# Two fused model blocks: every SBUF tile moved to a whole line of 64 bytes, with shared buffers for queries and values

## The chip, the cores and the metric

The kernel runs on one core of a Trainium2 chip. The metric is the device time of one execution in microseconds (us). The time before is the median of three runs: 1470.78 us (1470.22 to 1472.76).

## The reference

Two blocks follow each other, in float32, on 256 tokens of width 1024, with 16 meta tokens ahead of them.

```python
# first block
proj = rms_norm(h, g) @ w_in                      # 1024 -> 5 * 512
y_sc = bg * conv3(cg * xv)
y_cf = silu(layer_norm(conv31(ga * sigmoid(gg)) + b))
h = h + concat(rms_norm(y_sc), rms_norm(y_cf)) @ w_out
q = rms_norm(h) @ w_q                             # 8 heads, two halves of 128
...                                               # top 16 of 128 x 128 experts by head, softmax gates
act = gelu(u_sel . x);  h = h + (act * gates) @ v_sel
# second block
sb_q, sb_k, sb_v, df_q, df_k, df_v = split(rmsnorm(h) @ w_in2)
...                                               # stick-breaking and differential attention, 8 heads each
h = h + (gates0 * (o_sb @ w_br_sb) + gates1 * (o_df @ w_br_df)) @ w_out2
h = h + (silu(hn @ w_fg) * (hn @ w_fu)) @ w_fd    # 22 slices of 128
```

The kernel computes all 16384 experts densely (`u` and `v` have 128 chunks of 128 rows each) and multiplies the activations by a gate matrix that is zero outside of the chosen ones.

## The kernel before, in words

**Weights and units.** All weights come in units of 128 x 1024 float32 (512 KB). SyncE loads a unit into one of five `raw` buffers (line 128), ScalarE rounds it to float32r as `hi` (line 150), VectorE computes the rest `lo = raw - hi` (line 152); `hi` and `lo` have three buffers each. A product is then three float32r matmuls: hi by hi, hi by lo, lo by hi.

**Two forms of product.** `mm_w` (lines 164 to 171) takes the unit as the stationary operand and the activations as the moving one: 8 chunks x 3 = 24 matmuls, each of 128 x 128 weights, with 256 moving columns (272 where the meta tokens count too). `mm_a` (lines 173 to 184) takes the activations as stationary and half a unit as moving: 12 matmuls of 512 columns. Counted from the loops:

- 512 columns: units of `v` (128), `w_fd` (22), `w_out` (8), `w_out2` (8), 12 matmuls each: 1536 + 456 = 1992.
- 256 columns with `hThi`/`hTlo` as moving operand: `u` (128), `w_q` (16), `w_fg` and `w_fu` (44): 188 units x 24 = 4512.
- 256 columns with other moving operands: gates (16), queries (16), the two branches (16, moving operands `osb` and `odf`), `bg` (4): 52 x 24 = 1248.
- 272 columns: `gg`, `ga`, `cg`, `xv` (16), keys and values (32): 48 x 24 = 1152.

Together 8904 of the 10096 matmul instructions. The others are plain float32: transposes, the convolution (`conv`, line 373), the gate matrix (`gp`, line 675), attention scores and sums (`z`, `S`, `po`). A plain float32 matmul is two instructions in the trace.

**Order.** TensorE and SyncE run in the order in which the program is written; a scheduler orders the other engines. While the expert units of `u` run, VectorE routes the tokens and later builds the gate matrix (about 390 to 590 us). `v` follows (600 to 945 us), then the second block.

**SBUF.** Tiles come from pools. `const` (line 55) lives to the end; each phase opens a pool of its own with `phase` (line 63), in whose space the next phase puts its tiles. A tile has the same address in all 128 partitions. In the program before, each tile is given the bytes that it needs in a partition, rounded up to 32, and the tiles lie one behind the other. `const` begins at a multiple of 64 with `vec`, `ones` and `eps`; `eps` is one float32, so that it takes 32 bytes, and what lies behind it begins 32 bytes past a multiple of 64. Of the 207 different places of tiles in this program 184 lie so and 23 at a multiple of 64. All moving operands of the 8904 float32r matmuls are among the 184, and all their stationary operands but those of 48 (the second half of `w_out`).

**Attention.** `feat` (line 882) makes queries, keys and transposed values, `value` (line 894) transposes a head's values back. Queries have the tags `sq` and `dq` with two buffers each, values `sv` and `dv` with two each, for the two kinds of attention, which run one after the other (lines 1008 and 1032).

Of the kernel before, what the change touches and what calls it, by code (L numbers as in the profile page):

```python
# [8 lines left out]
F32 = mybir.dt.float32  # L9
# [9 lines left out]
P = 128  # L19
# [27 lines left out]
NV = _n  # L47


@with_exitstack  # L50
def two_blocks(ctx, tc, x, feats, vecs, w_in, w_out, w_q, keys, u, v, final_g, meta2, w_in2, lams, w_gate,
               w_br_sb, w_br_df, w_out2, w_fg, w_fu, w_fd, final_g2, gains, out):
    nc = tc.nc

    const = ctx.enter_context(tc.tile_pool(name="const", bufs=1))
    wraw = ctx.enter_context(tc.tile_pool(name="wraw", bufs=5))
    whi = ctx.enter_context(tc.tile_pool(name="whi", bufs=3))
    wlo = ctx.enter_context(tc.tile_pool(name="wlo", bufs=3))
# [3 lines left out]

    def phase(name):
        st = ExitStack()
        pool = st.enter_context(tc.tile_pool(name=name, bufs=1, reuse_waits="tile"))
        return st, pool

    def mm_tile(name):
        return pmm.tile([P, 512], F32, tag="mm", name=name)
# [3 lines left out]
    def at_tile(name):  # L73
        turn[0] += 1
        return pacc.tile([P, 512], F32, tag=f"a{turn[0] % 4}", name=name)
# [88 lines left out]
    def mm_w(ps, a, cols):  # L164
        hi, lo = unit()
        ahi, alo = a
        for k in range(KC):
            ks = slice(k * P, (k + 1) * P)
            nc.tensor.matmul(ps, hi[:, ks], ahi[:, k, cols], start=(k == 0), stop=False)  # L169
            nc.tensor.matmul(ps, hi[:, ks], alo[:, k, cols], start=False, stop=False)  # L170
            nc.tensor.matmul(ps, lo[:, ks], ahi[:, k, cols], start=False, stop=(k == KC - 1))  # L171
# [125 lines left out]
    sq = pc.tile([P, KC, L], F32, tag="sq", name="sq")  # L297
# [423 lines left out]
    for hd in range(NH):  # L721
# [3 lines left out]
        for half in range(2):  # L725
            ps = mm_tile(f"q{hd}{half}")
            mm_w(ps[:, :T], hT, slice(0, T))
            q = pr.tile([P, T], F32, tag="qT", name=f"qT{hd}{half}", bufs=4)
# [115 lines left out]
    QS = slice(NM, L)  # L844
# [37 lines left out]
    def feat(name, hd, tag, cols, scale=1.0):  # L882
        width = cols.stop - cols.start
        ps = mm_tile(f"ps_{name}")
        mm_w(ps[:, :width], xT2, cols)

        def scaled():
            o = padded[tag][hd % len(padded[tag])] if tag in padded else psb.tile([P, width], F32, tag=tag, name=name, bufs=2)
            nc.vector.scalar_tensor_tensor(o[:, :width], ps[:, :width], scale, rsb[:, cols], op0=ALU.mult, op1=ALU.mult)
            return o  # L890

        return scaled

    def value(name, tag, vt):
        ps = at_tile(f"pv_{name}")
        o = psb.tile([P, 3, P], F32, tag=tag, name=name, bufs=2)
        for kt in range(3):
            nc.tensor.transpose(ps[:, kt * P:(kt + 1) * P], vt[:, kt * P:(kt + 1) * P], ident)
        nc.scalar.activation(o, ps[:, :KP].rearrange("p (a b) -> p a b", a=3), AF.Copy)
        return o  # L900

    def qcols(kt, j=None):
        j = kt if j is None else j
        return slice(QO[kt] + Q0[j] - Q0[kt], QO[kt] + QN[kt])

    def stick(hd, q, k, vT):
        pz = at_tile(f"z{hd}")
        for kt in range(3):
            nc.tensor.matmul(pz[:, qcols(kt)], k[:, kt * P:(kt + 1) * P], q[:, Q0[kt]:], start=True, stop=True)
        z = psb.tile([P, NQ], F32, tag="z", name=f"zs{hd}", bufs=2)  # L910
        nc.vector.tensor_tensor(z, pz[:, :NQ], mneg, op=ALU.add)
        e = psb.tile([P, NQ], F32, tag="e", name=f"e{hd}", bufs=2)
        nc.scalar.activation(e, z, AF.Abs)
        nc.scalar.activation(e, e, AF.Exp, scale=-1.0)
        nc.scalar.activation(e, e, AF.Ln, bias=1.0)
        nc.vector.scalar_tensor_tensor(e, z, 0.0, e, op0=ALU.max, op1=ALU.add)
        yield
        vt = value(f"sv{hd}", "sv", vT)
        yield
        yield  # L920
        ps = at_tile(f"S{hd}")
        for kt in range(3):
            for j in range(kt, 3):
                nc.tensor.matmul(ps[:, qcols(kt, j)], tri if j == kt else ones, e[:, qcols(j)],
                                 start=(j == kt), stop=(j == 2))
        nc.vector.tensor_tensor(z, z, ps[:, :NQ], op=ALU.subtract)
        nc.scalar.activation(z, z, AF.Exp)
        yield
        yield
        po = at_tile(f"po{hd}")  # L930
        for kt in range(3):
            nc.tensor.matmul(po[:, Q0[kt]:T], vt[:, kt, :], z[:, qcols(kt)], start=(kt == 0), stop=(kt == 2))
        nc.scalar.activation(osb[0][:, hd, :], po[:, :T], AF.Copy)
        nc.vector.tensor_tensor(osb[1][:, hd, :], po[:, :T], osb[0][:, hd, :].bitcast(F32), op=ALU.subtract)
# [3 lines left out]
    def diff(hd, q, k, vT):  # L938
        slope = 2.0 ** (-(hd + 1))
        ws = []  # L940
        for t in range(2):
            kn = KN[t]
            nm = psb.tile([P, 2], F32, tag="nm", name=f"nm{hd}{t}", bufs=2)
            sm = psb.tile([P, 2], F32, tag="dsm", name=f"dsm{hd}{t}", bufs=2)
            pe = []
            for c in range(2):
                cs = slice(64 * c, 64 * c + 64)
                ps = at_tile(f"ds{hd}{t}{c}")
                nc.tensor.matmul(ps[:, :kn], q[cs, t * P:(t + 1) * P], k[cs, :kn], start=True, stop=True)
                s = psb.tile([P, kn], F32, tag=f"ds{t}{c}", name=f"dss{hd}{t}{c}", bufs=2)  # L950
                nc.vector.scalar_tensor_tensor(s, dist[t], -slope, ps[:, :kn], op0=ALU.mult, op1=ALU.add)
                nc.vector.tensor_reduce(nm[:, c:c + 1], s, axis=AX.X, op=ALU.max, negate=True)
                nc.scalar.activation(s, s, AF.Exp, bias=nm[:, c:c + 1], accum_out=sm[:, c:c + 1])
                pe.append(s)
            nc.vector.reciprocal(sm, sm)
            nc.vector.tensor_scalar(pe[1], pe[1], sm[:, 1:2], lam, op0=ALU.mult, op1=ALU.mult)
            w = padded[f"w{t}"][0]
            nc.vector.scalar_tensor_tensor(w[:, :kn], pe[0], sm[:, 0:1], pe[1], op0=ALU.mult, op1=ALU.subtract)
            ws.append(w)
            if t == 0:  # L960
                yield
        vt = value(f"dv{hd}", "dv", vT)
        yield
        yield
        outs = []
        for t in range(2):
            nk = KW[t] // P
            pw = at_tile(f"pw{hd}{t}")
            wT = psb.tile([P, 3, P], F32, tag="wT", name=f"wT{hd}{t}", bufs=2)
            for i in range(nk):  # L970
                nc.tensor.transpose(pw[:, i * P:(i + 1) * P], ws[t][:, i * P:(i + 1) * P], ident)
            nc.scalar.activation(wT[:, :nk, :], pw[:, :KW[t]].rearrange("p (a b) -> p a b", a=nk), AF.Copy)
            outs.append(wT)
        yield
        for t, wT in enumerate(outs):
            nk = KW[t] // P
            po = at_tile(f"dpo{hd}{t}")
            for i in range(nk):
                nc.tensor.matmul(po[:, :P], wT[:, i, :], vt[:, i, :], start=(i == 0), stop=(i == nk - 1))
            nc.scalar.activation(od[t][:, hd, :], po[:, :P], AF.Copy)  # L980
# [22 lines left out]
    def advance():  # L1003
        for g in list(running):
            if next(g, running) is running:
                running.remove(g)

    for hd in range(NH):
        q = feat(f"sq{hd}", hd, "sq", QS, float(P) ** -0.5)
        if hd > 0:  # L1010
            q = q()
            advance()
        k = feat(f"sk{hd}", hd, "k", FULL)
        if hd > 0:
            k = k()
            advance()
        else:
            with tc.high_priority(offset=20):
                cols = x2_norm()
        vT = feat(f"svT{hd}", hd, "vT", FULL)  # L1020
        if hd == 0:
            with first():
                across(pb, cols, rsb[:, QS], "rsb")
            tc.keep_in_program_order(nc.scalar.preload_act_table_set("natural_log_exp_and_others"))
            q, k = q(), k()
        running.append(stick(hd, q, k, vT()))
        if hd > 0:
            advance()
        if hd == 0:
            with queued([latest["hi"], latest["lo"]]):  # L1030
                small_parts()
    for hd in range(NH):
        q = feat(f"dq{hd}", hd, "dq", QS, 0.125)()
        advance()
        k = feat(f"dk{hd}", hd, "k", FULL)()
        advance()
        vT = feat(f"dvT{hd}", hd, "vT", FULL)()
        running.append(diff(hd, q, k, vT))
        advance()
# [160 lines left out]
```

## Time and profile before

| | |
|---|---|
| median of the runs | 1470.78 us |
| the profiled execution | 1472.7 us |
| its span, first to last instruction | 1470.5 us |
| mean granted TensorE clock | 0.993 |
| busy: TensorE, its weight loads | 1440.7, 1341.6 us |
| busy: VectorE, ScalarE, GpSimd | 1052.5, 737.6, 14.7 us |
| DMA | 248.95 MB, mean 169 GB/s |

A matmul's duration in the trace includes its way through the array, and the next one starts before it ends. What a matmul costs in a row of matmuls is therefore the distance from its start to the next start, called its pace below: the starts of two rows, divided by the number of matmuls from the one to the other. The timeline gives starts to 0.01 us, so that a pace over 10 to 30 matmuls is good to about 1 ns. Two levels of the TensorE clock occur, 2.4 GHz (granted 1.00) and 1.2 GHz (0.50).

### The profile page before, as it was taken

What the parts mean: (1) busy time and instruction counts of PE and PEld (TensorE: products, weight loads), DVE (VectorE), ACT (ScalarE), POOL (GpSimd) and SP (SyncE); (2) the same over time, 40 slices, a digit from 0 to 9 for tenths busy, and PEclk for the clock granted to TensorE, in tenths of its full rate; (3) what the DMA queues carried; (4) which work ended last, traced back from release to release, by engine and by line L of the source; (5) the groups of instructions that cost most, each with busy time, mean ns of one, the idle gap of its engine ahead of it and who ended that gap; (6) DMA issues with size and microseconds to landing.
All of it is one profiled execution on the core that took longest, in us unless ns stands there. A gap on an engine that the chain in (4) does not pass through costs nothing.

```text
span 1470.5 us, 25555 instructions
## 1 busy us (share of the span) xinstructions
PE 1440.7 (98%) x10096; PEld 1341.6 (91%) x10096; DVE 1052.5 (72%) x1888; ACT 737.6 (50%) x1216; POOL 14.7 (1%) x35
## 2 busy tenths in 40 slices
PE   8999999999999999899999999999999999999998
PEld 7988999999999999688888888799999999899997
DVE  8987669679788999655555555665577776766665
ACT  7555444445444444244444444554455674544444
POOL 0010000000000000000000000100000000000000
PEclk9999999999999999999999999999999999999999
DMA  7525665665544444366666676553444455566562
GB/s 235 201 73 186 194 190 175 204 189 169 176 144 144 143 138 138 106 194 198 191 193 193 198 245 192 180 160 127 129 129 130 129 172 187 167 190 189 186 188 99
DMA packets 69815, 248.95 MB, mean 169 GB/s; under 512 B 7744, under 2 KB 9152, under 8 KB 69696
## 3 DMA queue, kind: packets, MB, share of 16 engines
q1 hardware_dynamic: 68544, 243.13, 52.6%
q0 software_dynamic: 1152, 4.19, 0.8%
q8 instruction: 79, 1.29, 0.4%
q14 instruction: 40, 0.33, 0.1%
HBM read 245.20 MB, written 2.10 MB: 168 GB/s over the span
## 4 chain that ended last, share of the span: by engine, by line
PE 94%; DVE 3%; DMA 1%; issue 1%; ACT 0%; SPq 0%; POOL 0%; DVEq 0%; ACTq 0%
PE u L171 8%; PE u L169 8%; PE u L170 8%; PE v L184 8%; PE v L183 8%; PE v L182 8%; PE gp L675 4%; PE fg L170 1%; PE fu L171 1%; PE fg L171 1%; PE fd L184 1%; PE fu L170 1%; PE fu L169 1%; PE fg L169 1%; PE fd L183 1%; PE fd L182 1%
## 5 line engine op out<-in xcount | busy, mean ns | idle before, releaser
L152 DVE TENSOR_TENSOR lo<-raw,hi 128x1024 fp32r<-128x1024 f32 x453 | 553.6, 1224 | 243.6 <-ACT hi L150 241.9
L150 ACT ACTIVATE hi<-raw 128x1024 fp32r<-128x1024 f32 x453 | 479.0, 1059 | 467.6 <-PE u L170 123.7
L169 PE MATMUL u<-hThi,hi 128*128 128x256 f32 x1024 | 290.5, 284 | 0.0
L171 PE MATMUL u<-hThi,lo 128*128 128x256 f32 x1024 | 285.7, 279 | 0.1
L170 PE MATMUL u<-hTlo,hi 128*128 128x256 f32 x1024 | 285.5, 279 | 0.0
L182 PE MATMUL v<-hi,w_hi 128*128 128x512 f32 x512 | 200.5, 392 | 1.3 <-ACT w_hi L764 1.3
L184 PE MATMUL v<-hi,w_lo 128*128 128x512 f32 x512 | 200.6, 392 | 0.5 <-DVE w_lo L766 0.5
L183 PE MATMUL v<-lo,w_hi 128*128 128x512 f32 x512 | 200.3, 391 | 0.1
L170 PEld LDWEIGHTS u<-hTlo,hi 128*128 128x128 f32 x1024 | 194.7, 190 | 0.0
L171 PEld LDWEIGHTS u<-hThi,lo 128*128 128x128 f32 x1024 | 192.2, 188 | 0.3 <-DVE lo L152 0.3
L169 PEld LDWEIGHTS u<-hThi,hi 128*128 128x128 f32 x1024 | 192.5, 188 | 0.0
L182 PEld LDWEIGHTS v<-hi,w_hi 128*128 128x128 f32 x512 | 96.8, 189 | 21.6 <-ACT w_hi L764 1.5
L184 PEld LDWEIGHTS v<-hi,w_lo 128*128 128x128 f32 x512 | 96.8, 189 | 21.3 <-DVE w_lo L766 1.0
L183 PEld LDWEIGHTS v<-lo,w_hi 128*128 128x128 f32 x512 | 96.8, 189 | 20.5 <-DVE lo L152 0.5
L675 PE MATMUL gp<-ga,gb 128*128 128x128 f32 x512 | 66.6, 275 | 4.0 <-DVE gb L666 4.0
L764 ACT ACTIVATE w_hi<-ewa 128x512 fp32r<-128x512 f32 x48 | 30.3, 633 | 77.4 <-PE v L183 66.7
L675 PEld LDWEIGHTS gp<-ga,gb 128*128 128x128 f32 x512 | 61.7, 191 | 4.8 <-PE gp L675 3.6
L766 DVE TENSOR_TENSOR w_lo<-ewa,w_hi 128x512 fp32r<-128x512 f32 x48 | 33.2, 693 | 39.4 <-ACT w_hi L764 39.4
L662 DVE TENSOR_TENSOR ga<-o,o 128x512 f32<-128x512 f32 x64 | 44.1, 689 | 17.7 <-PE gp L675 17.3
L170 PE MATMUL fg<-hTlo,hi 128*128 128x256 f32 x176 | 49.2, 279 | 0.5 <-DVE hTlo L223 0.5
L169 PE MATMUL fg<-hThi,hi 128*128 128x256 f32 x176 | 49.3, 280 | 0.3 <-ACT hThi L222 0.3
L171 PE MATMUL fu<-hThi,lo 128*128 128x256 f32 x176 | 49.1, 279 | 0.0
(407 smaller groups left out, 2957.3 us busy)
## 6 DMA issues: line engine op xcount, KB each, us to landing
raw<-in_u_dram SPq DMA_DIRECT2D x128, 512.0 KB, 3.6
raw<-in_v_dram SPq DMA_DIRECT2D x128, 512.0 KB, 3.6
raw<-in_w_in_dram SPq DMA_DIRECT2D x67, 512.0 KB, 3.6
raw<-in_w_fg_dram SPq DMA_DIRECT2D x22, 512.0 KB, 3.5
raw<-in_w_fu_dram SPq DMA_DIRECT2D x22, 512.0 KB, 3.5
raw<-in_w_fd_dram SPq DMA_DIRECT2D x22, 512.0 KB, 3.5
raw<-in_w_out_dram SPq DMA_DIRECT2D x16, 512.0 KB, 3.5
raw<-in_w_q_dram SPq DMA_DIRECT2D x16, 512.0 KB, 4.2
```

The lines of the kernel that those rows point to most:

```text
L150: latest["hi"] = nc.scalar.activation(hi, loaded[i], AF.Copy)
L152: latest["lo"] = nc.vector.tensor_tensor(lo, loaded[i], hi.bitcast(F32), op=ALU.subtract)
L169: nc.tensor.matmul(ps, hi[:, ks], ahi[:, k, cols], start=(k == 0), stop=False)
L170: nc.tensor.matmul(ps, hi[:, ks], alo[:, k, cols], start=False, stop=False)
L171: nc.tensor.matmul(ps, lo[:, ks], ahi[:, k, cols], start=False, stop=(k == KC - 1))
L182: nc.tensor.matmul(ps, ahi[:, ts], hi[:, bs], start=first and n == 0, stop=False)
L183: nc.tensor.matmul(ps, ahi[:, ts], lo[:, bs], start=False, stop=False)
L184: nc.tensor.matmul(ps, alo[:, ts], hi[:, bs], start=False, stop=end)
L662: nc.vector.tensor_tensor(a.rearrange("p t (h l) -> p t h l", h=8), o8[:, tl, :].unsqueeze(3).broadcast_to((P, 4, 8, TOPK)), o16[:, tl, :] ...
L675: nc.tensor.matmul(p3[:, :, i], b[:, i, :], a[:, i, :], start=True, stop=True)
L764: nc.scalar.activation(hi, a, AF.Copy)
L766: nc.vector.tensor_tensor(lo, a, hi.bitcast(F32), op=ALU.subtract)
```

## The change: tiles at multiples of 64 bytes

A class `Lines` stands between the kernel and the pools `const` and those of the phases. A tile whose bytes in a partition are no multiple of 64 is made longer: where it has two dimensions it is allocated longer and cut to its shape, else a small tile is put behind it. So each tile begins at a multiple of 64. (The pools of the weights, whose tiles have 4096 bytes, are as before, but lie behind `const`.) Queries of both kinds of attention get the tag `q`, values the tag `vt`, with two buffers each, so that the four tags `sq`, `dq`, `sv`, `dv` become two.

```diff
+LINE = 64
+class Lines:
+    def __init__(self, pool):
+        self.pool, self.seen = pool, set()
+
+    def tile(self, shape, dtype, tag, name, **kw):
+        size = 4
+        for n in shape[1:]:
+            size *= n
+        odd = -size % LINE
+        if odd and len(shape) == 2:
+            return self.pool.tile([shape[0], shape[1] + odd // 4], dtype, tag=tag, name=name, **kw)[:, :shape[1]]
+        t = self.pool.tile(shape, dtype, tag=tag, name=name, **kw)
+        if odd and tag not in self.seen:
+            self.pool.tile([P, odd // 4], F32, tag=f"{tag}_end", name=f"{tag}_end")
+        self.seen.add(tag)
+        return t
...
-    const = ctx.enter_context(tc.tile_pool(name="const", bufs=1))
+    const = Lines(ctx.enter_context(tc.tile_pool(name="const", bufs=1)))
...
-        pool = st.enter_context(tc.tile_pool(name=name, bufs=1, reuse_waits="tile"))
+        pool = Lines(st.enter_context(tc.tile_pool(name=name, bufs=1, reuse_waits="tile")))
...
-        vt = value(f"sv{hd}", "sv", vT)
+        vt = value(f"sv{hd}", "vt", vT)
...
-        vt = value(f"dv{hd}", "dv", vT)
+        vt = value(f"dv{hd}", "vt", vT)
...
-        q = feat(f"sq{hd}", hd, "sq", QS, float(P) ** -0.5)
+        q = feat(f"sq{hd}", hd, "q", QS, float(P) ** -0.5)
...
-        q = feat(f"dq{hd}", hd, "dq", QS, 0.125)()
+        q = feat(f"dq{hd}", hd, "q", QS, 0.125)()
```

On all five engines the instructions of the two programs are the same, in the same order, with the same operands but for their addresses. The waits are the same too, but for one: GpSimd's second `kpad` memset (line 880 before) now waits for TensorE. Of the 207 places of tiles 205 are now multiples of 64. `hThi` and `hTlo` lie 32 bytes further than before (behind `eps`), `raw`, `hi` and `lo` 96 bytes (behind `eps`, `lam` and `sg8`), `osb` 416. The distance from the stationary to the moving operand of a matmul, taken by 256 bytes, so goes from 192 to 128 where `hT` moves over `hi` or `lo`, and from 128 to 192 where `osb` or `odf` does.

## Rows read from the trace of the kernel before

**Rows 1.** The page: the span, busy time of each engine, the chain.
```profile
span 1470.5 us, 25555 instructions
PE 1440.7 (98%) x10096; PEld 1341.6 (91%) x10096; DVE 1052.5 (72%) x1888; ACT 737.6 (50%) x1216; POOL 14.7 (1%) x35
PE 94%; DVE 3%; DMA 1%; issue 1%; ACT 0%; SPq 0%; POOL 0%; DVEq 0%; ACTq 0%
```
**Rows 2.** Timeline, TensorE, `v` at full clock: start, us, what.
```profile
660.11 0.39 PE L182 MATMUL v<-hi,w_hi 128*128 128x512 f32 x1
...
665.55 0.39 PE L182 MATMUL v<-hi,w_hi 128*128 128x512 f32 x1
```
**Rows 3.** The same at the beginning of `v`.
```profile
603.43 0.63 PE L183 MATMUL v<-lo,w_hi 128*128 128x512 f32 x1
...
605.99 0.63 PE L183 MATMUL v<-lo,w_hi 128*128 128x512 f32 x1
```
**Rows 4.** Busy time by stretch; behind POOL: granted clock, DMA share, GB/s.
```profile
603.90:606.50 2.60, 2.60 (x8) 2.02 (x7) 0.00 (x0) 0.69 (x1) 0.00 (x0) 0.50 0.00 0
660.00:665.00 5.00, 5.00 (x24) 4.15 (x23) 2.80 (x3) 2.58 (x3) 0.00 (x0) 1.00 0.61 193
```
**Rows 5.** Timeline, TensorE, `u`: two stretches.
```profile
279.96 0.28 PE L169 MATMUL u<-hThi,hi 128*128 128x256 f32 x1
...
281.32 0.28 PE L169 MATMUL u<-hThi,hi 128*128 128x256 f32 x1
...
298.94 0.28 PE L169 MATMUL u<-hThi,hi 128*128 128x256 f32 x1
...
302.12 0.28 PE L169 MATMUL u<-hThi,hi 128*128 128x256 f32 x1
```
**Rows 6.** Timeline, TensorE: 272 columns, `ysb`, `fd`.
```profile
990.26 0.29 PE L171 MATMUL ps_svT<-xT2hi,lo 128*128 128x272 f32 x1
...
991.40 0.29 PE L171 MATMUL ps_svT<-xT2hi,lo 128*128 128x272 f32 x1
...
1208.81 0.28 PE L169 MATMUL ysb<-osbhi,hi 128*128 128x256 f32 x1
...
1210.95 0.28 PE L169 MATMUL ysb<-osbhi,hi 128*128 128x256 f32 x1
...
1321.00 0.39 PE L182 MATMUL fd<-hi,f_hi 128*128 128x512 f32 x1
...
1323.09 0.39 PE L182 MATMUL fd<-hi,f_hi 128*128 128x512 f32 x1
```
**Rows 7.** Timeline, TensorE, plain float32: the convolution of one channel group.
```profile
67.40 13.55 PE L373 MATMUL conv<-up,diag 128*128 128x256 f32 x62
```
**Rows 8.** Timeline, TensorE, plain float32 with 16 columns.
```profile
993.71 0.37 PE L924 MATMUL S<-e,tri 128*128 128x16 f32 x2
993.93 1.05 PE L909 MATMUL z<-sq,kpad 128*128 128x256 f32 x6
```
**Rows 9.** By stretch: `u` alone, and `u` with the gate matrix.
```profile
200.00:390.00 190.00, 189.85 (x1637) 189.43 (x1637) 153.80 (x404) 94.52 (x144) 0.00 (x0) 1.00 0.59 186
400.00:600.00 200.00, 194.66 (x1688) 193.66 (x1688) 184.55 (x345) 85.20 (x229) 0.00 (x0) 1.00 0.44 135
```
**Rows 10.** Groups by line, weight loads of `w_out`: 95.5 to 107, 110 to 122 us.
```profile
L182 PEld LDWEIGHTS wo<-hi,yhi 128*128 128x128 f32 x12 | 2.3, 188 | 0.5
...
L182 PEld LDWEIGHTS wo<-hi,yhi 128*128 128x128 f32 x11 | 2.1, 188 | 0.5
```
**Rows 11.** VectorE's taps of the convolution: duration ns min/median/max.
```profile
L355 DVE SCALAR_TENSOR_TENSOR cf<-up,vec,cf x79: 475/484/500, 23.3 to 82.7; 128x256 f32<-128x256 f32 x79
```
**Rows 12.** Timeline, GpSimd: the memsets of the padded tiles.
```profile
945.55 0.31 POOL L880 MEMSET kpad<- 128x112 f32 x2
945.81 0.18 POOL L880 MEMSET vTpad<- 128x112 f32 x1
```

## Prediction

> **What bounds the kernel now.** I read the page first, then the chain, then the timeline of TensorE in each stage. TensorE is busy for 1440.7 of 1470.5 us and holds 94% of the chain of waits [rows 1]; nothing else has more than 3%. So a change that leaves the instructions and their order alone can only act where it makes the matmuls themselves, or something that TensorE already waits for, quicker or slower. Time off VectorE, ScalarE or the DMAs is worth at most the 30 us in which TensorE is idle.
>
> The question is then what a matmul costs, and the timeline answers it. In `v`, 24 matmuls of 512 columns go from 660.11 to 665.55 us: a pace of 226.7 ns [rows 2]. At the granted clock of 1.00, 2.4 GHz [rows 4], 512 columns at one a cycle would take 213.3 ns. 226.7 ns is 544 cycles: 512 and a sixteenth of it. In `u`, 12 matmuls of 256 columns take 1.36 us, 113.3 ns each [rows 5]: 272 cycles, again 256 and a sixteenth. A sixteenth is one cycle in 16 columns, and 16 columns of four bytes are 64 bytes. Two rows say what kind of cost that is. At the beginning of `v`, where the clock is granted at 0.50 (1.2 GHz) [rows 4], six of the same matmuls go from 603.43 to 605.99 us: 426.7 ns each [rows 3], which is 512 cycles with nothing on top. And the plain float32 matmuls of the convolution, which need two cycles for a column (two instructions, 256 columns each), come at (13.55 - 0.38) / 61 = 215.9 ns [rows 7], 518 cycles for 512: no sixteenth either. So the extra cycle appears only where the array takes four bytes a cycle at the full clock: the operand is not brought quickly enough, by one cycle in every 64 bytes. And every one of these moving operands begins 32 bytes past a multiple of 64.
>
> Three more things stand in the rows. The same `u` matmul also runs at 3.18 us / 27 = 117.8 ns [rows 5]; with 272 columns the pace is 1.14 us / 9 = 126.7 ns, in `ysb` 2.14 us / 18 = 118.9 ns, in `fd` 2.09 us / 9 = 232.2 ns [rows 6]. A second cost of some 5 ns comes and goes. Over 190 us of `u` and queries the mean is 190 us / 1635 = 116.2 ns (of 1637 counted, two reach over the edges) [rows 9]. [...]
>
> **The change part by part.** *The shared buffers.* Queries and values of the second attention begin when those of the first are two heads old, and no engine has a new wait from it. Cost 0. *The one new wait.* GpSimd's second `kpad` memset waits for TensorE; the next instruction of the queue, the `vTpad` memset at 945.81 us [rows 12], waits for TensorE already, so nothing is queued behind it that did not wait before. Cost 0; if it were not covered, one memset, under 0.2 us.
>
> *Addresses of what VectorE, ScalarE and the weight load read.* The trace has its own test. The 79 taps of the convolution on VectorE read `up` from starts that go on by 4 bytes, over all places in a line, and take 475 to 500 ns, median 484 [rows 11]. The weight loads of `w_out` take 188 ns with a stationary operand 32 bytes past a line (first half) and 188 ns at a whole line (second half) [rows 10]. So I take 0 for both, between -0.5% and +0.5% of 1052 us of VectorE, of which next to nothing is on the path.
>
> *Addresses of the moving operands.* Here the trace has no second case: all 8904 float32r matmuls have the same offset. I bound the cost from both sides. One bound is that nothing happens, 0. The other is that the sixteenth goes and with it the second cost of 5 ns, down to the floors that the rows show: 215.9 ns for 512 columns (the pace of the convolution), 114.7 ns for 272 (its half, by 272/256), 110 ns for 256 (the weight load, which is above the half, 108). By the counts of the loops:
> - `v`: 1536 x (226.7 - 215.9) = 16.6 us;
> - the other 512 columns: 456 x (232.2 - 215.9) = 7.4 us;
> - 272 columns: 1152 x (126.7 - 114.7) = 13.8 us;
> - 256 columns over `hT`: 4512 x (116.2 - 110) = 28.0 us;
> - 256 columns over the others, at the pace of `ysb`: 1248 x (118.9 - 110) = 11.1 us.
>
> Sum 76.9 us. If the second cost stays and the sixteenth alone goes: 1992 x 10.8 = 21.5 us, 272 columns from 17/16 (120.4 ns) to 114.7, 1152 x 5.7 = 6.6 us, 256 columns from 113.3 to 110, 5760 x 3.3 = 19.0 us; sum 47.1 us. The nearest rows are those of `v` and of the quick `u`, where the sixteenth stands alone; so I take 47.1 and only a quarter of the difference, 7.5. From 400 to 600 us VectorE is busy for 184.55 of 200 us [rows 9], and TensorE waits for it there; that stage will give back some of its share, say 3 us. Forecast: 51.5 us less.
>
> The profiled execution took 1472.7 us, 2.2 more than its span, and the median of the runs is 1.9 below it. 1472.7 - 51.5 - 1.9 = 1419 us.
>
> **The rivals.** *Same: the sixteenth is the supply's own.* One cycle in 64 bytes may be what a full-rate float32r stream costs at any address. [...] Time: 1471 us. [...]
>
> *Slower: the second cost follows the distance of the operands.* The paces of 113.3 and 117.8 ns for one and the same matmul say that the weight load and the moving stream, which run at the same time, meet. Distance from stationary to moving operand, taken by 256 bytes: 192 for `u`, mean 116.2 ns [rows 9]; 128 for `ysb`, 118.9 ns throughout [rows 6]; 0 for `v`, where there is no second cost. With the change `hT` gets 128 and `osb` and `odf` get 192. If the sixteenth stays and the distance decides, 4512 matmuls go to 118.9 ns, + 4512 x 2.7 = 12.2 us, and 384 come back by as much, - 1.0 us: 1482 us. This decides only if alignment gives nothing. Against it: `u` shows both paces at one distance. [...]
>
> *A little faster: the second cost goes, the sixteenth stays.* All 4512 at 113.3 ns, - 13.1 us, and 456 at 226.7, - 2.5 us: 1455 us. For it: `v` and half of `u` run so already; against it, nothing says why the new addresses should be the good ones.
>
> **How the numbers follow.** The forecast gets 0.42, the same time 0.20, slower 0.22 and a little faster 0.16. The forecast's own range is 1394 (76.9 us) to 1443 us (only 512 and 272 columns gain, 28 us). A difference of less than 0.2% (3 us) can't be told from none. Faster is 0.42 + 0.16 = 0.58 less 0.01 for a small gain, 0.57; same 0.20; slower 0.23 with a little for mishaps. For 8 in 10 I leave out most of the slower case and the far end of the forecast: 1403 to 1477 us.
>
> **What the profile after would show.** If I am right, the pace of `v` falls from 226.7 ns to about 216, that of `u` to 110 to 113, that of 272 columns to about 116, everywhere in the kernel alike, and the busy time of TensorE falls as much as the span, while VectorE's and ScalarE's durations stay as they are. The first stage to show another bound would be that of the gate matrix, with VectorE above 95% and longer waits of TensorE for `gb`. I am wrong if `v` still runs at 226.7 ns: then the sixteenth is no matter of lines, and what the time does is read from the share of `u` matmuls at 113.3, 117.8 and 118.9 ns.

## The result, and the profile after

The changed kernel takes 1481.26 us (median of 4 runs, 1480.87 to 1483.21), against 1470.50 us for the kernel before (median of 4, three of them those of the median given above). The ratio is 1.0078, 95% interval 1.0056 to 1.0100: slower by 0.56% to 1.0%. The forecast was 1419 us, with a range of 1403 to 1477 us. What came true is the slower rival, which gave 1482 us.

The page of the kernel after, span, busy time and chain, as in [rows 1]:

```profile
span 1478.8 us, 25555 instructions
PE 1449.9 (98%) x10096; PEld 1353.2 (92%) x10096; DVE 1052.7 (71%) x1888; ACT 738.4 (50%) x1216; POOL 15.8 (1%) x35
PE 95%; DVE 3%; ACT 1%; issue 0%; DMA 0%; SPq 0%; ACTq 0%; DVEq 0%
```

The span is 8.3 us longer and TensorE is busy for 9.2 us more; VectorE and ScalarE stand still. So the time was added in TensorE's own matmuls, as the whole argument supposed, but with the other sign. The timeline of TensorE (start, us, what) says which; every line of the changed kernel has a number 23 higher than before, so that L192 is L169 and L205 is L182:

```profile
280.04 0.28 PE L192 MATMUL u<-hThi,hi 128*128 128x256 f32 x1
...
283.24 0.28 PE L192 MATMUL u<-hThi,hi 128*128 128x256 f32 x1
...
520.06 0.29 PE L192 MATMUL u<-hThi,hi 128*128 128x256 f32 x1
...
522.22 0.29 PE L192 MATMUL u<-hThi,hi 128*128 128x256 f32 x1
...
610.99 0.50 PE L205 MATMUL v<-hi,w_hi 128*128 128x512 f32 x1 [1.31 <-ACT w_hi L787]
...
660.21 0.39 PE L205 MATMUL v<-hi,w_hi 128*128 128x512 f32 x1
...
665.65 0.39 PE L205 MATMUL v<-hi,w_hi 128*128 128x512 f32 x1
...
1215.61 0.28 PE L192 MATMUL ysb<-osbhi,hi 128*128 128x256 f32 x1
...
1216.97 0.28 PE L192 MATMUL ysb<-osbhi,hi 128*128 128x256 f32 x1
```

- `v`: 24 matmuls in 5.44 us, 226.7 ns, the same as in [rows 2]. The sixteenth did not move.
- `u`: 27 matmuls in 3.20 us, 118.5 ns, and later 18 in 2.16 us, 120.0 ns. The paces of 113.3 and 117.8 ns of [rows 5] are gone.
- `ysb`: 12 matmuls in 1.36 us, 113.3 ns, where [rows 6] had 118.9.

`u` and `ysb` have changed places, as their distances did. The windows of [rows 9] show the same by counts: of `u` and queries 1597 matmuls fit into 190 us, and 1637 before.

```profile
200.00:390.00 190.00, 190.00 (x1597) 190.00 (x1596) 149.91 (x399) 92.58 (x140) 0.00 (x0) 1.00 0.60 184
400.00:600.00 200.00, 200.00 (x1699) 199.81 (x1697) 178.89 (x328) 87.62 (x234) 0.00 (x0) 1.00 0.44 136
```

The account, in differences of start-to-start distances summed over each product (waits included), after less before: `u` +10.7 us, `w_fg` and `w_fu` +3.0, `w_q` +1.2; `ysb` and `ydf` -1.9, the other products of 512 columns -1.4 and `v` -3.3. Sum +8.3 us, which is the difference of the spans. `v` gained nothing in pace: before, it began like this

```profile
599.87 0.50 PE L182 MATMUL v<-hi,w_hi 128*128 128x512 f32 x1 [1.31 <-ACT w_hi L764]
...
601.73 0.63 PE L182 MATMUL v<-hi,w_hi 128*128 128x512 f32 x1
...
607.27 0.41 PE L183 MATMUL v<-lo,w_hi 128*128 128x512 f32 x1
```

and the 13 matmuls from 601.73 to 607.27 us, 426 ns each, ran at a granted clock of 0.50 [rows 3, 4]: 13 x 0.2 = 2.6 us of the 3.3. After, it begins 11.1 us later, which is what had been lost up to there, and at the full clock. That the 3.3 us come from the change is not shown, since executions of one kernel differ by as much: the kernel before took 1466.2 to 1468.0 us in executions with a mean granted clock of 0.998 and 1473.9 to 1475.0 us in those with 0.992 (0.993 in the one profiled), and in the sixteen traces of this case between 0 and 13 matmuls of `v` run at 0.50. After, the dip of the clock lies ahead of `v`, on matmuls of `gp`:

```profile
603.00:606.00 3.00, 2.87 (x13) 2.60 (x14) 3.00 (x8) 0.00 (x0) 0.00 (x0) 0.55 0.00 0
```

Eleven of them take some 214 ns each instead of 112, but the waits for `gb` are fewer: the waits of TensorE from 400 us to the beginning of `v` (waited for, us, times, longest), before and after,

```profile
PE gp L675 <- DVE gb L666: 4.0, 5, 1.1
```

```profile
PE gp L698 <- DVE gb L689: 2.5, 3, 1.1
```

and the sum over `gp`, waits included, is 59.7 us before and 59.9 after. So the waits took up the dip. Of the loss in `u` they took up nothing: in e2, e5 and e9 below, where `u` is as slow and no `gp` runs at the low clock of 0.50, TensorE waits for `gb` 4.0 us in 5 waits, as before.

### The profile page after: what moved, and what is told of

The parts are those of the page before. It is cut to its first block, busy times and chain, and to the rows that moved or that the text cites. A ratio compares the mean times of both kernels' runs of the same rounds, so it can differ in the third digit from the quotient of the medians.

```text
span 1478.8 us, 25555 instructions
## 1 busy us (share of the span) xinstructions
PE 1449.9 (98%) x10096; PEld 1353.2 (92%) x10096; DVE 1052.7 (71%) x1888; ACT 738.4 (50%) x1216; POOL 15.8 (1%) x35
## 4 chain that ended last, share of the span: by engine, by line
PE 95%; DVE 3%; ACT 1%; issue 0%; DMA 0%; SPq 0%; ACTq 0%; DVEq 0%
PE u L192 8%; PE u L194 8%; PE u L193 8%; PE v L207 8%; PE v L206 8%; PE v L205 8%; PE gp L698 3%; PE fg L193 1%; PE fu L194 1%; PE fu L192 1%; PE fu L193 1%; PE fg L192 1%; PE fg L194 1%; PE fd L207 1%; PE fd L205 1%; PE fd L206 1%
## 5 line engine op out<-in xcount | busy, mean ns | idle before, releaser
L192 PE MATMUL u<-hThi,hi 128*128 128x256 f32 x1024 | 295.2, 288 | 0.0
L194 PE MATMUL u<-hThi,lo 128*128 128x256 f32 x1024 | 290.5, 284 | 0.0
L193 PE MATMUL u<-hTlo,hi 128*128 128x256 f32 x1024 | 290.5, 284 | 0.0
L205 PE MATMUL v<-hi,w_hi 128*128 128x512 f32 x512 | 199.3, 389 | 1.3 <-ACT w_hi L787 1.3
L192 PEld LDWEIGHTS u<-hThi,hi 128*128 128x128 f32 x1024 | 194.4, 190 | 0.0
L205 PEld LDWEIGHTS v<-hi,w_hi 128*128 128x128 f32 x512 | 96.1, 188 | 21.4 <-ACT w_hi L787 1.5
L192 PE MATMUL fg<-hThi,hi 128*128 128x256 f32 x176 | 49.7, 283 | 0.3 <-ACT hThi L245 0.3
```

The lines of the kernel that those rows point to most:

```text
L205: nc.tensor.matmul(ps, ahi[:, ts], hi[:, bs], start=first and n == 0, stop=False)
```

## The experiments

The kernels that change addresses do it with unused tiles, most of them with a single one beside `hThi` and `hTlo`, which moves what lies behind it: `raw`, `hi` and `lo`. So the distance from `hi` (stationary) to `hT` (moving) is set; with a single such tile no instruction, order or wait changes (in e9 and e14 a few waits do, and in e14 the order on ScalarE in places). "Distance" means the moving operand's address less the stationary one's, taken by 256 bytes. The pace of `u` is the mean of the start-to-start distances under 135 ns of its matmuls (some 3000 of 3072).

| kernel | distance of `hT` | us | ratio to before, 95% | `u`, ns |
|---|---|---|---|---|
| before | 192 | 1470.50 | | 115.8 |
| after | 128 | 1481.26 | 1.0056 to 1.0100 | 119.6 |
| e1_shared_only | 192 | 1468.54 | 0.9991 to 1.0012 | 115.7 |
| e2_before_gap64 | 128 | 1486.74 | 1.0093 to 1.0134 | 120.0 |
| e3_after_gap192 | 192 | 1465.44 | 0.9963 to 0.9983 | 116.1 |
| e4_after_ahead64 | 128 | 1481.25 | 1.0066 to 1.0100 | 119.5 |
| e5_after_gap128 | 0 | 1483.67 | 1.0085 to 1.0111 | 119.9 |
| e6_after_gap64 | 64 | 1475.27 | 1.0025 to 1.0049 | 117.7 |
| e7_after_gap32 | 96 | 1484.19 | 1.0087 to 1.0113 | 119.9 |
| e9_all_zero | 0 | 1486.28 | 1.0103 to 1.0133 | 119.9 |
| e10_other256 | 192 | 1466.27 | 0.9967 to 0.9988 | 115.8 |
| e11_after_gap224 | 160 | 1476.78 | 1.0033 to 1.0063 | 118.0 |
| e12_after_gap160 | 224 | 1478.18 | 1.0034 to 1.0075 | 118.4 |
| e13_half_loads | 128 | 1469.86 | 0.9982 to 1.0014 | 116.6 |
| e14_steady_xT | 192 | 1466.97 | 0.9968 to 0.9992 | 115.8 |
| e15_half_loads_192 | 192 | 1456.21 | 0.9895 to 0.9928 | 113.6 |

The ratios of the runs with an e are to runs of the kernel before on the same chip (medians of 1468.4 to 1469.8 us there). e13 and e15 leave out part of the computation.

**One part alone: the shared buffers.**

```diff
 # in the kernel before
-        vt = value(f"sv{hd}", "sv", vT)
+        vt = value(f"sv{hd}", "vt", vT)
 # ... and so for dv, sq, dq
```

> The kernel before with the shared tags for queries and values alone: no tile of const, of the weights or of hT moves, only tiles of the second block's attention and what lies behind them. Distance theory (what counts is the distance from the stationary to the moving operand of a matmul, taken by 256 bytes): no distance of a float32r matmul changes, so 1470.5 us as before, within 3 us. Rival, the shared buffers make a wait in the attention: 1475 to 1481 us with u at its old paces of 113.3 and 117.8 ns.

The ratio is 1.0002 (0.9991 to 1.0012): this part costs nothing, and all else is addresses.

**The distance without the alignment, and the alignment without the distance.**

```diff
 # e2: in the kernel before (no alignment); e3: in the kernel after
+    const.tile([P, 16], F32, tag="gap", name="gap")    # e2, behind hT
+    const.tile([P, 48], F32, tag="gap", name="gap")    # e3, behind hT
```

> The kernel before, unaligned as it was, with one unused tile of 64 bytes behind hTlo: raw, hi, lo and all later tiles move by 64 bytes, hT stays. The distance over hT goes from 192 to 128, no other one changes. Distance theory: u, q, fg and fu go to a pace of 119 to 120 ns, 4512 x 3 to 3.5 ns, so 1482 to 1486 us; ysb stays at 118.9. Rival, tiles at whole lines of 64 bytes are what slows the moving operand: none is aligned here, so 1470.5 us.

> The changed kernel with one unused tile of 192 bytes behind hTlo: all tiles stay at multiples of 64, the distance over hT goes back from 128 to 192, that over osb and odf stays 192. Distance theory: u, q, fg and fu come back to a mean of 113.3 to 116 ns, 4512 x 3 to 6 ns less than 1481, so 1454 to 1468 us. Rival, alignment itself costs: 1481 us.

The two decide it. In e2 no tile is aligned that was not, but `hT` has distance 128, and the kernel is 1.1% slower; in e3 all tiles are aligned and `hT` is back at 192, and it is 0.27% faster than before. (e2 lies 0.7 us over its range; e3 is in its own.) TensorE's timeline, e2, 18 matmuls in 2.16 us, 120.0 ns:

```profile
280.54 0.29 PE L169 MATMUL u<-hThi,hi 128*128 128x256 f32 x1
...
282.70 0.29 PE L169 MATMUL u<-hThi,hi 128*128 128x256 f32 x1
```

and e3:

```profile
135.01 0.28 PE L192 MATMUL u<-hThi,hi 128*128 128x256 f32 x1
...
138.19 0.28 PE L192 MATMUL u<-hThi,hi 128*128 128x256 f32 x1
...
139.36 0.37 PE L192 MATMUL u<-hThi,hi 128*128 128x256 f32 x1
139.80 0.28 PE L192 MATMUL u<-hThi,hi 128*128 128x256 f32 x1
140.14 0.28 PE L192 MATMUL u<-hThi,hi 128*128 128x256 f32 x1
...
142.52 0.28 PE L192 MATMUL u<-hThi,hi 128*128 128x256 f32 x1
```

Here both old paces stand next to each other: 27 matmuls in 3.18 us, 117.8 ns, and then 21 from 140.14 to 142.52 us, 113.3 ns. Between them the matmul of 139.36 us, the first of a unit, has 0.37 us instead of 0.28, and from it to 139.80 us three starts take 0.44 us instead of 0.35: a pause of some 90 ns, and behind it the stream runs at the other pace. At distance 192 there are two steady states, and a pause throws the stream from one to the other: of e3's 66 stretches of 12 or more `u` matmuls that no pause and no other product breaks, none changes its pace inside; 33 run at 113.3 to 114.0 ns and 33 at 117.8, and from one stretch to the next the state changes 59 times out of 65. So the mean of `u` at this distance lies about midway.

**The address itself, and how far it counts.**

```diff
 # e4: the same tile of 64 bytes ahead of hT: all behind it moves, distance 128 as after
+    const.tile([P, 16], F32, tag="gap", name="gap")
 # e10: distance 192 as in e3, but 256 bytes less between the two
+    lam = const.tile([P, 1], F32, tag="lam", name="lam")      # ahead of hT, no more behind it
+    sg8 = const.tile([P, 1], F32, tag="sg8", name="sg8")
     hT = ...
+    const.tile([P, 16], F32, tag="gap", name="gap")
```

> The changed kernel with one unused tile of 64 bytes ahead of hThi: hT and all later tiles move together, so that the address of the moving operand, taken by 256 bytes, goes from 192 to 0 and no distance changes. Distance theory: 1481 us, u at 119 to 120 ns as in the changed kernel. Rival, the address of the moving operand itself counts: another pace of u, by 2 ns or more, 10 us or more off 1481.

> The changed kernel with lam and sg8 ahead of hT and one unused tile of 64 bytes behind it: the distance over hT is 192 by 256 bytes, as in the run with 192 bytes behind hTlo, but 256 bytes away from that one's, so another distance by 512 bytes. If the distance counts by 256 bytes or less: 1465 us, u at 113.3 and 117.8 ns. Rival, it counts by 512 bytes or more: 1470 to 1484 us with another pace.

With `hT` moved by 64 bytes but its distance kept, e4 takes 1481.25 us, the time of the kernel after; e10 takes that of e3. Nor does the address of the weights count by itself: in e4, e6 and e10 `hi` has the same address, and `u` has 119.5, 117.7 and 115.8 ns. So the addresses do not count, the distance does, and by 256 bytes or a part of it.

**The other distances.** The tile behind `hT` has 128, 64, 32, 224 and 160 bytes (the last three give distances that are no multiple of 64).

> The changed kernel with one unused tile of 128 bytes behind hTlo: the distance over hT goes from 128 to 0, no other one changes. Distance theory: 0 is the distance of v, which shows 17/16 of the columns and nothing more, so u, q, fg and fu at 113.3 ns throughout, 4512 x 5 to 6 ns less than 1481: 1453 to 1459 us. Rival, 192 alone is good and any other distance costs as 128 does: 1481 us.

> The changed kernel with one unused tile of 64 bytes behind hTlo: the distance over hT goes to 64, no other one changes. Distance theory, if the cost grows and falls steadily from 0 over 128 to 192: u between 113.3 and 119.5 ns, 1460 to 1472 us. If what counts is the distance by 128 bytes alone, 64 would do as 192 does in the run with 192: 1465 us. Rival, any distance but 192 costs as 128 does: 1481 us.

> The changed kernel with one unused tile of 32 bytes behind hTlo: hT stays at whole lines, raw, hi, lo and all later tiles begin 32 bytes past a line, the distance over hT is 96. Distance theory: no new cost from the half line itself; v still at 226.7 ns; u between its paces at 64 and 128, or, if half lines meet in two places, as slow as at 128 or slower: 1465 to 1485 us. Rival, whole lines are what counts: v leaves 226.7 ns, since its operands are at half lines now.

> The changed kernel with one unused tile of 224 bytes behind hTlo: distance over hT 160, all that lies behind hT 32 bytes past a line. Between 128 (119.5 ns, 1481 us) and 192 (115.7 ns, 1465 us) by the distance theory if cost is steady in the distance, so 1470 to 1478 us; if a half line always costs, as 96 did, 1484 us.

> The changed kernel with one unused tile of 160 bytes behind hTlo: distance over hT 224, all that lies behind hT 32 bytes past a line. Between 192 (1465 us) and 0 (1484 us): 1470 to 1480 us by a cost that is steady in the distance; 1484 us if a half line always costs.

e5 is a miss: I had read from `v`, which runs without a second cost at distance 0, that 0 is free. It is as bad as any. 27 matmuls of `u` in 3.24 us, 120.0 ns, without a break:

```profile
280.16 0.28 PE L192 MATMUL u<-hThi,hi 128*128 128x256 f32 x1
...
283.40 0.28 PE L192 MATMUL u<-hThi,hi 128*128 128x256 f32 x1
```

e6 has one steady pace too, 21 matmuls in 2.47 us, 117.6 ns:

```profile
280.05 0.28 PE L192 MATMUL u<-hThi,hi 128*128 128x256 f32 x1
...
282.52 0.28 PE L192 MATMUL u<-hThi,hi 128*128 128x256 f32 x1
```

e6 is a miss too: its time, 1475.27 us, is that of none of its three cases. e7, e11 and e12 lie in their ranges, but the cost is not steady in the distance: `u` has 119.9, 117.7, 119.9 and 119.6 ns at 0, 64, 96 and 128. Since 64 and 192 differ, and 96 and 224, the distance does not count by 128 bytes.

The order is 192 (best), then 64, 160, 224, and 96, 128 and 0 (119.5 to 120.0 ns). Of the seven distances 192 alone reaches 113.3 ns for long stretches. It happened to be that of the kernel before.

**All distances of 256 and 512 columns at 0.**

```diff
 # beside e5's tile: gaps ahead of the buffers of osb, of the slices of w_fd and of ysq
+    pq.tile([P, 16], F32, tag="gap_o", name="gap_o")
+    pf_.tile([P, 32], F32, tag="gap_f", name="gap_f")
+        pc.tile([P, (32, 48)[br]], F32, tag=f"gap_y{br}", name=f"gap_y{br}")
```

> The changed kernel with unused tiles of 128 bytes behind hTlo, 64 ahead of osb, 128 ahead of f_hi, 128 and 192 ahead of the two halves of yhi: all distances of float32r matmuls with 256 and 512 columns are 0, but for those over xT and xT2, whose rows of 1088 bytes go through 0, 64, 128 and 192. Distance theory: the saving of the run with 128 bytes behind hTlo alone and of 456 matmuls of 512 columns that go from some 231 to 226.7 ns, 2 us: 1451 to 1457 us. Rival, 512 columns do not care: the same as that run.

e9 is a miss for the reason of e5: 1486.28 us. `ysb` follows: 27 matmuls in 3.24 us, 120.0 ns, after 113.3 at distance 192.

```profile
1217.34 0.28 PE L192 MATMUL ysb<-osbhi,hi 128*128 128x256 f32 x1
...
1220.58 0.28 PE L192 MATMUL ysb<-osbhi,hi 128*128 128x256 f32 x1
```

The matmuls of 512 columns do like 0: `fd` has a mean of 228.7 ns there, against 231.3 to 233.3 in the kernels with 128 and 232.3 to 232.9 in those with 192. The two shapes want different distances, so that "0 is free" held for `v` only.

**Does the weight load meet the moving stream?** `mm_w`'s hi-by-lo and lo-by-hi matmuls, but the last of a unit, load 64 of 128 stationary columns (134 ns in the trace instead of 188); left out are these corrections for the upper half of the outputs. e13 is the kernel after with this, e15 is e3 with it.

```diff
-            nc.tensor.matmul(ps, hi[:, ks], alo[:, k, cols], start=False, stop=False)
-            nc.tensor.matmul(ps, lo[:, ks], ahi[:, k, cols], start=False, stop=(k == KC - 1))
+            nc.tensor.matmul(ps[:64], hi[:, k * P:k * P + 64], alo[:, k, cols], start=False, stop=False)
+            n = P if k == KC - 1 else 64
+            nc.tensor.matmul(ps[:n], lo[:, k * P:k * P + n], ahi[:, k, cols], start=False, stop=(k == KC - 1))
```

> The changed kernel, in which hi by lo and lo by hi of each matmul of mm_w but the last of a group take 64 of the 128 stationary columns; it leaves out these corrections for the upper half of each output. Distances stay as in the changed kernel (128 over hT). If it is the weight load that meets the moving stream, two of three loads are half as long and the second cost shrinks or goes: u at 113.3 to 115.5 ns and 272 columns at 120.4 to 122, 5760 x 4 to 6 ns and 1152 x 4 to 6 ns, 1442 to 1455 us. Rival, the moving stream alone has the second cost, by its own place: 1481 us. In both the sixteenth stays, and no pace of 256 columns falls under 113.3 ns.

> The tiles aligned and hT at distance 192, and all lo-by-hi and hi-by-lo matmuls of mm_w but the last of a unit load only 64 of the 128 stationary columns (the upper half of their output is not corrected, so that part of the computation is left out). If what is left over 113.3 ns at distance 192 is the weight load meeting the moving stream, the half load shrinks the stretches at 117.8 ns: u below 115 ns on average, and 1455 to 1462 us. If the half load only breaks the regular meeting at a bad distance (as it took u from 119.5 to 117 to 118 ns at distance 128), it leaves u at 117 to 118 ns here too, worse than with whole loads, and the time at 1468 to 1471 us.

e13 came out between its two cases: 11.4 us less than after, not 26 to 39 less. e15 came out at the weight load's case. The moving columns and their number are the same in both, and yet at distance 192 the state of 117.8 ns is gone. TensorE's timeline of e15 behind a pause, 36 matmuls in 4.08 us, 113.3 ns:

```profile
285.28 0.36 PE L192 MATMUL u<-hThi,hi 128*128 128x256 f32 x1
...
285.72 0.28 PE L192 MATMUL u<-hThi,hi 128*128 128x256 f32 x1
...
289.80 0.28 PE L192 MATMUL u<-hThi,hi 128*128 128x256 f32 x1
```

and its windows, where 1662 matmuls fit into the 190 us that held 1637 before:

```profile
200.00:390.00 190.00, 189.53 (x1662) 188.07 (x1661) 155.56 (x396) 95.21 (x144) 0.00 (x0) 1.00 0.62 191
```

So what the matmuls of `hT` pay above 113.3 ns shrinks with the load, by 3.0 ns (of 6.3) at distance 128 and by nearly all (2.5 of 2.8) at 192. That fits a meeting of weight load and moving stream, as does the distance between the two, which decides the pace (e2 to e4, e10). It does not prove that the load's length is the cause: with the loaded columns the rows of the output are halved as well, and no run here separates the two. At 113.3 ns the gain ends: the sixteenth is no part of it.

**Other moving operands.** The chunks of `xT` and `xT2` were 1088 bytes apart, so that their distance went through 0, 64, 128 and 192.

```diff
-    xT = (pc.tile([P, KC, L], F32R, tag="xThi", name="xThi"), pc.tile([P, KC, L], F32R, tag="xTlo", name="xTlo"))
+    pc.tile([P, 48], F32, tag="gap_xT", name="gap_xT")
+    xT = tuple(pc.tile([P, KC, 320], F32R, tag="xT" + e, name="xT" + e)[:, :, :L] for e in ("hi", "lo"))
 # ... and so for xT2, without a gap; e3's tile behind hT
```

> The tiles aligned, hT at distance 192 (as in the run at 192 before), and the tiles xT and xT2, whose chunks were 1088 bytes apart (so that their distance went through 0, 64, 128 and 192 from chunk to chunk), now have chunks 1280 bytes apart: distance 192 throughout for the 256 columns of queries and gates and for the 272 columns of the first block (gg, ga, cg, xv), 128 throughout for the 272 columns of keys and values. If the distance decides for every moving operand: queries and gates fall from 118.5 to about 115.7 ns or into a pattern of 113 and 118 (768 matmuls, -2.1 us), gg to xv from 126 to 120.4 to 125 ns (384 matmuls, -0.4 to -2 us), keys and values rise to 119.5 x 17/16 = 127 ns (768 matmuls, +0.8 us): 1462 to 1465 us, the fastest of all. If it decides for hT alone, the paces of these stay at 118.5 and 126 ns and the time at 1465 to 1466 us.

Its timeline, first block and second (272 columns at distance 192, then 256 at 192):

```profile
30.22 0.29 PE L192 MATMUL gg<-xThi,hi 128*128 128x272 f32 x1
...
32.81 0.28 PE L192 MATMUL gg<-xThi,hi 128*128 128x272 f32 x1
...
979.03 0.28 PE L192 MATMUL ps_sq<-xT2hi,hi 128*128 128x256 f32 x1
...
981.07 0.28 PE L192 MATMUL ps_sq<-xT2hi,hi 128*128 128x256 f32 x1
```

The law holds for them: `gg` falls to 2.59 / 21 = 123.3 ns (mean of `gg` to `xv` 123.4, before 126.1), this stretch of queries to 2.04 / 18 = 113.3 ns, and keys and values, at 128, rise from 125.8 to 126.6, as does `bg`, now at 0, from 117.3 to 119.8. But the time, 1466.97 us, does not fall under that of e3, and lies 1 to 2 us over both ranges: the mean of queries and gates is 117.1 ns (118.1 in e3), because most of them fall into the state of 117.8 ns, and `ysb` and `ydf`, whose distance is still 192, go from 113.8 to 116.7 in the mean, into the mixture of both states. What the distance allows is not always reached.

e3, e10 and e14, which leave nothing out, are faster than both kernels: by 0.27% (0.17% to 0.37%), 0.23% and 0.20% than before.

## Why the prediction was wrong

**What bounds the kernel** was right. TensorE had 94% of the chain and has 95%; a change that only moves addresses acted through the matmuls alone. VectorE's taps have a median of 477 to 484 ns in all sixteen kernels, and they, the shared buffers (e1) and GpSimd's wait cost nothing, as put. Two other terms were wrong. The 0 for the addresses of the weight loads holds for their duration (188 to 192 ns), but not for the matmuls: e3 moves `raw`, `hi` and `lo` by 192 bytes, and takes 15.8 us less than after. And the stage of the gate matrix gives back nothing of a change in `u`, where I had 3 us: TensorE waits there for `gb` 4.0 us whether `u` has 113.6 ns (e15) or 120.0 (e2).

**The step that failed is "Addresses of the moving operands"**, with 47.1 us for the sixteenth and 7.5 for a part of the second cost. The reading behind it, one cycle in 64 bytes because the operand begins amid a line of 64, did not hold: 16 columns of 4 bytes are 64 bytes, but nothing in the trace tied the cycle to the place where an operand begins. `v` has 226.7 ns in all sixteen kernels, aligned and not (256 columns keep their 113.3 too, in `ysb` after and in e15), so the sixteenth gave 0 and not 47.1 us, and the second cost, which goes by the distance of the two operands and not by lines, grew by 11.6 us instead of shrinking by 7.5. In e7, whose `hT` and `hi` differ by half a line, `u` has 119.9 ns, as in e5, which keeps whole lines. That the operand is brought too slowly no run shows. I had named the gap in the step (no second offset among 8904 matmuls in the trace), and still gave it 0.42.

Two figures of the forecast rest on less than it says. The rows give the clock as a share; 2.4 GHz for 1.00 is an estimate from [rows 3, 4], where 512 columns in 426.7 ns at 0.50 are 1.2 columns per ns, counted as one a cycle. So "nothing on top" at 0.50 is a way of counting; what the rows show is 226.7 ns at 1.00 against 213.3, the half of 426.7. And the 110 ns for 256 columns no run shows as the time of a weight load: the loads of `u` have 187 to 193 ns in the traces of before, after and e5 (200 to 390 us), the two matmuls of 16 columns ahead of those of [rows 8], each with a load, take 0.14 us up to the next start at 993.71 us, 70 ns each in the mean, and no steady pace of 256 columns came out under 113.3 ns.

```profile
993.57 0.29 PE L924 MATMUL S<-e,ones 128*128 128x16 f32 x2
```

The rival *same* was right on the alignment: the 2.9 us that e3 takes off with `hT` at its old distance are explained by the products whose distance did change (in its trace `ysb` and `ydf` -1.9 us, the 512 columns but `v` -1.3).

The rival *slower* was right that the distance decides, and nearly in size: 1482 us forecast, 1481.26 measured. Its price, 4512 x 2.7 = 12.2 us less 1.0, came out as 14.9 less 1.9, and 1.4 more came back in products of 512 columns, which I had not counted: 11.6 us. The medians lie 10.8 us apart; e4, with the distances of the kernel after, lies 12.9 over the kernel before on its chip. That the end agrees to 1 us is in part luck. What spoke against it, that `u` shows both paces at one distance, was no objection: a distance allows one state (0, 64) or two (192), and pauses choose between them. The rows had told more than I took: `ysb`, with no pace but 118.9 at distance 128, was the second case that the trace offered.

Its reading, that weight load and moving stream meet, fits two more results: the pace of `u` goes by the distance between the two operands (120.0 ns in e2 against 115.8 before, 116.1 in e3 against 119.6 after), and halving the loaded columns takes 9 to 11 us off (e15 against e3, e13 against after) with the same moving operands, though with fewer rows of output.

What stays open: why distances that differ by 256 bytes give the same pace (e3 and e10, `u` at 116.1 and 115.8 ns); why 512 columns do better at 0 (`fd`, 228.7 ns against 231.3 to 233.3); what the sixteenth is. It seems no part of the weight load, since it grows with the columns (226.7 less 213.3 is 13.4 ns in 512, 113.3 less 106.7 is 6.6 in 256, with one load each) and stays with half loads (113.3 ns in e15). Nor was a load taken away altogether, or shortened with the output left whole. In e6, e12 and e13 `fd` went from 231.4 to 233.1 and 233.3 ns with its distance unchanged, which the distance alone does not explain.

## What to carry to other kernels

Where TensorE is the bound and each matmul has a weight load of its own, read the pace of the same matmul in several places of the timeline: several paces for one shape were here the sign that the places of weights and stream matter, and then a few bytes of padding between the two tiles are worth a try, some 1.4% between best and worst here. A tidy address was no gain in itself here (1481.26 us against 1470.50): aligning tiles moves every distance, and a tuned kernel may sit on a good one by chance, so lay out again by the pace. A cost that fits a number (a sixteenth, 64 bytes) is not explained by it; look for a second case in the trace before giving it weight.

## What the runs showed of the hardware

- float32r matmuls of 256 columns, each with a load of 128 x 128, take 113.3 to 120.0 ns at a granted clock of 1.00, by the distance of stationary and moving operand taken by 256 bytes. `u` has 119.9 at 0 (e5, e9), 117.7 at 64 (e6), 119.9 at 96 (e7), 119.5 to 120.0 at 128 (after, e2, e4), 118.0 at 160 (e11), 113.3 and 117.8 in turn, from pause to pause, at 192 (e3), and 118.4 at 224 (e12).
- Those of 512 columns follow it less: 226.7 ns (`v`, 0), `fd` 228.7 at 0 (e9), 231.3 to 233.3 at 128 (after 231.4), 232.3 to 232.9 at 192 (before 232.9).
- The quickest pace of float32r at 1.00 is 17/16 of half of what a column takes at 0.50: 226.7 ns for 512 columns [rows 2] and 113.3 for 256 [rows 5], against 426.7 for 512 at 0.50 [rows 3]. An instruction of plain float32 with 256 columns has 215.9 ns [rows 7], near 213.3, the half of those 426.7.
